# A two-block kernel on one core: expert fetches with a shorter lag, routing deferred, query columns in two parts

## The chip, the cores and the metric

The kernel runs on one core of one Trainium2 chip. The metric is the device time of one execution in microseconds (us). The engines are PE (matrix products), DVE (vector), ACT (scalar functions), POOL (which here mostly issues the indexed fetches) and SP (which issues the weight loads).

## The reference

Two transformer blocks over 256 tokens of 2048 channels, in float32. The change concerns the feed-forward part at the end of the first one, in which every token fetches 128 rows from each of two tables of 16384 rows:

```python
    q = (hf @ w_q).reshape(t, PEER_HEADS, 2, PEER_HALF).astype(jnp.float32)
...
    s1 = jnp.einsum('thd,nd->thn', q[:, :, 0], sk[0])
    s2 = jnp.einsum('thd,nd->thn', q[:, :, 1], sk[1])
    v1, i1 = lax.top_k(s1, PEER_TOPK)
    v2, i2 = lax.top_k(s2, PEER_TOPK)
    cand = (v1[..., :, None] + v2[..., None, :]).reshape(t, PEER_HEADS, PEER_TOPK * PEER_TOPK)
    cs, ci = lax.top_k(cand, PEER_TOPK)
    row = jnp.take_along_axis(i1, ci // PEER_TOPK, axis=-1)
    col = jnp.take_along_axis(i2, ci % PEER_TOPK, axis=-1)
    experts = row * PEER_NKEYS + col
    gates = jax.nn.softmax(cs, axis=-1)
...
        a = jax.nn.gelu(jnp.einsum('chkd,cd->chk', expert_u[ec], hc).astype(jnp.float32))
        w = (gc * a).astype(hc.dtype)
        return jnp.einsum('chk,chkd->cd', w, expert_v[ec])
```

Here `hf` is the normalized row (`h2` in the kernel), `w_q` is 2048 x 2048 (8 heads, two halves of 128 each), there are 128 keys to a half, PEER_TOPK is 16, and a row of `expert_u` or `expert_v` has 2048 floats. All of it is added to the residual, and the second block follows.

## The kernel before

Tokens stand on the 128 partitions, in two tiles t = 0 and 1. Every dense layer streams its weights in parts of 512 KB through four `raw` buffers (SP issues the loads in program order, `prep`, L106). ACT rounds a part to a high half (L109), DVE subtracts it to get the low half (L110), and PE makes each product of three of the faster float32r kind (L166 to L168): high x high, high x low, low x high. `h2` is kept in the same two halves, written by `split_evac` (L224 to L226). The four buffers that hold a split part are the `hl` buffers.

The first block ends with `w_out1`. Then comes `peer`: `w_qp` (the 2048 query columns) is a dense layer of 4 blocks of 512 columns, two heads to a block, 8 parts to a block. As a block ends, `ev_qp` evacuates it, transposes it (L216), multiplies it with the keys (L740) and gets 4 x 128 scores per token. For t = 0 the generator `route` follows at once, on DVE: top-16 of each 128 (L666 to L670), top-16 of the 256 sums, the row number in `ef` and, cast, in `eidx` (L717), the softmax, and a transposed copy of the row numbers in `eidv` (L680). For t = 1 the scores are kept in `gslot[:, 3]` and routed late. A generator that yields is resumed one part of the dense later (`tick`), so that DVE's rows of routing and of splitting alternate in its queue.

The fetches are indirect DMAs issued by POOL (L786), in the order of the list `seq`. A first-table fetch takes one row of `expert_u` for each of the 128 tokens of a tile (slot k of head and rank), 1 MiB; its use (`use_u`, L812) is a dot product with `hrow` on DVE, which frees the slot. When 32 are used, `weights` makes the coefficients. A second-table fetch brings, for four tokens, 32 rows each of `expert_v`; its use (`use_v`, L828) is four products on PE with 32 weight columns, whose strips of tokens accumulate over 128 fetches. `VLAG` is the number of first-table fetches that stand in `seq` before the first second-table fetch; from there the two kinds alternate.

A fetch needs a free slot and, for the first table, a routed head (`ready`). Slots before: `gslot` 0 to 2 and the tile `gbc` (the gain of `h2`, which `hrow` is made with at L659); after the dense the four `hl` buffers, and `gslot` 3 when the late scores are done. `hook` calls `step` (issue, use) before every second part of the dense. Every engine works off its queue in order; the order is fixed when the program is built.

Of the kernel before, what the change touches and what calls it, by code (L numbers as in the profile page):

```python
# [22 lines left out]
P = 128  # L23
T = 256
# [15 lines left out]
VLAG = 36  # L40


class Builder:
# [49 lines left out]
    def add_plan(self, w):  # L93
        nb, kc, _, kk, n = w.shape
        step = 2 if n <= 512 else 1
        for b in range(nb):
            for c in range(kc):
                for k0 in range(0, kk, step):
                    self.plan.append((w[b, c][:, k0:min(kk, k0 + step)], min(step, kk - k0), n))
# [134 lines left out]
    def row_to_lhs(self, row, HI, LO, kt, t, n=4, gain=None, scale=1.0):  # L234
        ps = self.transpose4(row, n)
        s = slice(t * P, (t + 1) * P)
        self.split_evac(ps, HI[:, kt:kt + n, s], LO[:, kt:kt + n, s],
                        None if gain is None else gain[:, kt:kt + n], scale)
# [73 lines left out]
    def build(self):  # L312
        nc, d = self.nc, self.d
        for w in ("w_ckvq", "w_kr", "w_ukv", "w_uq", "w_dqkv", "w_gate", "w_oa", "w_out1", "w_qp"):
# [5 lines left out]
            else:  # L320
                self.add_plan(d[w])
# [25 lines left out]
    def block1(self):  # L347
# [267 lines left out]
        h2h, h2l = self.pair("B", F32R, "h2")  # L615
        ss2 = cst.tile([P, 2, 4], F32, tag="ss2", name="ss2")

        def ev_out(b, t, ps):
# [5 lines left out]
            self.row_to_lhs(xres[:, t, sl], h2h, h2l, 4 * b, t, 4, G("g_norm2"))  # L624
# [3 lines left out]
        self.h2 = lambda k, t: (h2h[:, k, t * P:(t + 1) * P], h2l[:, k, t * P:(t + 1) * P])  # L628
        s2 = self.stat_sum(ss2, "r2")
# [4 lines left out]
    def peer(self):  # L634
# [6 lines left out]
        vmask = self.cload("vmask", [P, 8, 32], pool=pp)  # L641
# [33 lines left out]
        def spread(dst, src, b, copy):  # L675
            tp = self.tr()
            nc.tensor.transpose(tp[:, :P], src, self.ident)
            tv = tp[32 * b:32 * b + 32, :P].rearrange("p (i m) -> p m i", m=4)
            for m in range(4):
                copy(dst[32 * m:32 * m + 32], tv[:, m])  # L680

        def route(b, t, sc):
            sl = slice(32 * b, 32 * b + 32)
            V = rt(64, "rt_v").rearrange("p (h w s) -> p h w s", h=2, w=2)
            I = rt(64, "rt_i", U32).rearrange("p (h w s) -> p h w s", h=2, w=2)
            for j in range(4):
# [3 lines left out]
            tab = rt(64, "rt_tab").rearrange("p (h w s) -> p h w s", h=2, w=2)  # L690
            nc.vector.tensor_copy(tab, I)
            nc.vector.tensor_scalar(tab[:, :, 0], tab[:, :, 0], float(P), None, op0=ALU.mult)
            cand = self.at([P, 2, 16, 16])
            nc.vector.tensor_tensor(cand, V[:, :, 0].unsqueeze(3).to_broadcast([P, 2, 16, 16]),
                                    V[:, :, 1].unsqueeze(2).to_broadcast([P, 2, 16, 16]), op=ALU.add)
            cs = rt(32, "rt_cs")
            ci = rt(32, "rt_ci", U32)
            for i in range(2):
# [609 lines left out]
```

## Time and profile before

| | before |
|---|---|
| median of 3 runs | 2880.39 us (2880.06 to 2881.32) |
| the profiled execution | 2880.4 us, span 2878.6 us |
| PE, DVE, ACT, POOL busy, share of the span | 80%, 58%, 27%, 23% |
| mean granted clock of PE | 0.904 |
| moved by DMA | 820.24 MB, 285 GB/s mean |

Shares are means over the whole span, which holds stages of different limits: products from 0 to about 700 us and from 2062 us on, fetches in between. A row of the table by stretches gives the length, then the busy time and the number of instructions of PE, PE's weight loads, DVE, ACT and POOL, the granted clock (1.00 is 2.4 GHz), the share of the 16 DMA engines that is busy, and GB/s.

### The profile page before, as it was taken

What the parts mean: (1) busy time and instruction counts of PE and PEld (TensorE: products, weight loads), DVE (VectorE), ACT (ScalarE), POOL (GpSimd) and SP (SyncE); (2) the same over time, 40 slices, a digit from 0 to 9 for tenths busy, and PEclk for the clock granted to TensorE, in tenths of its full rate; (3) what the DMA queues carried; (4) which work ended last, traced back from release to release, by engine and by line L of the source; (5) the groups of instructions that cost most, each with busy time, mean ns of one, the idle gap of its engine ahead of it and who ended that gap; (6) DMA issues with size and microseconds to landing.
All of it is one profiled execution on the core that took longest, in us unless ns stands there. A gap on an engine that the chain in (4) does not pass through costs nothing.

```text
span 2878.6 us, 26351 instructions
## 1 busy us (share of the span) xinstructions
PE 2307.9 (80%) x9488; PEld 1445.4 (50%) x9488; DVE 1679.5 (58%) x2503; ACT 791.2 (27%) x1245; POOL 668.8 (23%) x570
## 2 busy tenths in 40 slices
PE   9999999999515565556666666657899999999999
PEld 7878788888401111111111111111388888888887
DVE  5665755657999644444445444441365566667754
ACT  6544544444200000000000000000244444447743
POOL 0000000000354554445445353534100000001000
PEclk9999999999857878887787878788999999999999
DMA  7545466555989999999999999999755555553355
GB/s 249 171 146 183 151 225 199 185 187 194 353 325 357 407 422 421 422 421 421 422 421 422 422 421 422 422 421 421 290 193 188 170 172 188 187 174 131 121 183 168
DMA packets 151955, 820.24 MB, mean 285 GB/s; under 512 B 17232, under 2 KB 17264, under 8 KB 85776
## 3 DMA queue, kind: packets, MB, share of 16 engines
q0 software_dynamic: 75360, 543.75, 46.1%
q1 hardware_dynamic: 76464, 274.81, 28.5%
q8 instruction: 74, 1.21, 0.2%
q14 instruction: 57, 0.47, 0.0%
HBM read 816.39 MB, written 2.10 MB: 284 GB/s over the span
## 4 chain that ended last, share of the span: by engine, by line
PE 50%; DMA 22%; issue 14%; DVE 7%; POOL 7%; ACT 0%; SPq 0%; POOLq 0%; DVEq 0%; ACTq 0%
PE acc L167 15%; PE acc L166 15%; PE acc L168 15%; DMA hg<-expert_v,eidv 8%; DMA gslot<-expert_v,eidv 7%; DMA hj<-expert_v,eidv 3%; POOL gslot L786 3%; POOL hg L786 3%; DVE hj L812 2%; DMA gslot<-expert_u,eidx 2%; PE tr L216 1%; PE acc L828 1%; POOL hj L786 1%; DVE hl L110 1%; PE sd L1146 1%
## 5 line engine op out<-in xcount | busy, mean ns | idle before, releaser
L110 DVE TENSOR_TENSOR hl<-raw,hl 128x1024 fp32r<-128x1024 f32 (+1 forms) x516 | 623.3, 1211 | 525.7 <-ACT hl L109 525.2
L109 ACT ACTIVATE hl<-raw 128x1024 fp32r<-128x1024 f32 (+1 forms) x516 | 540.9, 1049 | 765.9 <-PE acc L168 630.7
L166 PE MATMUL acc<-hl,h 128*128 128x512 f32 (+1 forms) x1472 | 580.8, 395 | 3.4 <-ACT hl L109 3.4
L167 PE MATMUL acc<-hl,h 128*128 128x512 f32 (+1 forms) x1472 | 574.4, 390 | 9.7 <-DVE hl L110 9.7
L168 PE MATMUL acc<-hl,h 128*128 128x512 f32 (+1 forms) x1472 | 573.7, 390 | 0.0
L828 PE MATMUL acc<-hg,lw 128*32 128x512 f32 x880 | 410.2, 811 | 199.5 <-DMA hg<-expert_v,eidv 195.7
L828 PE MATMUL acc<-gslot,lw 128*32 128x512 f32 x848 | 413.0, 806 | 176.2 <-DMA gslot<-expert_v,eidv 176.0
L812 DVE CUSTOM_DVE_ANT_0 hj<-gslot,hj 128x2048 f16<-128x2048 f32 x121 | 277.2, 2291 | 239.5 <-DMA gslot<-expert_u,eidx 239.2
L812 DVE CUSTOM_DVE_ANT_0 hj<-hg,hj 128x2048 f16<-128x2048 f32 x116 | 265.6, 2290 | 205.7 <-DMA hg<-expert_u,eidx 205.3
L167 PEld LDWEIGHTS acc<-hl,h 128*128 128x128 f32 x1472 | 277.1, 188 | 70.0 <-DVE hl L110 13.6
L166 PEld LDWEIGHTS acc<-hl,h 128*128 128x128 f32 x1472 | 276.8, 188 | 61.8 <-ACT hl L109 5.0
L168 PEld LDWEIGHTS acc<-hl,h 128*128 128x128 f32 x1472 | 276.7, 188 | 57.3 <-issue 1.3
L828 PEld LDWEIGHTS acc<-hg,lw 128*32 128x32 f32 x880 | 79.9, 139 | 442.5 <-DMA hg<-expert_v,eidv 273.2
L828 PEld LDWEIGHTS acc<-gslot,lw 128*32 128x32 f32 x848 | 80.3, 138 | 398.5 <-DMA gslot<-expert_v,eidv 251.4
L828 PE MATMUL acc<-hj,lw 128*32 128x512 f32 x320 | 208.1, 803 | 89.5 <-DMA hj<-expert_v,eidv 89.4
L799 ACT ACTIVATE dots<-dots 128x32 f32<-128x32 f32 x8 | 1.8, 229 | 985.7 <-DVE dots L812 985.7
L204 POOL TENSOR_TENSOR rs_y<-rs_v,mhalf 128x2 f32<-128x2 f32 (+2 forms) x25 | 30.3, 1213 | 809.8 <-DVE rs_v L203 809.2
L786 POOL DMA_INDIRECT hg<-expert_v,eidv x110 | 141.9, 1290 | 169.7 <-PE acc L828 126.2
L786 POOL DMA_INDIRECT gslot<-expert_v,eidv x106 | 129.5, 1222 | 205.1 <-PE acc L828 165.3
L786 POOL DMA_INDIRECT gslot<-expert_u,eidx x121 | 131.3, 1085 | 184.6 <-issue 71.9
L786 POOL DMA_INDIRECT hg<-expert_u,eidx x116 | 138.8, 1196 | 128.6 <-DMA hg<-expert_v,eidv 29.1
L828 PEld LDWEIGHTS acc<-hj,lw 128*32 128x32 f32 x320 | 39.7, 139 | 194.1 <-DMA hj<-expert_v,eidv 118.9
(304 smaller groups left out, 2377.1 us busy)
## 6 DMA issues: line engine op xcount, KB each, us to landing
raw<-ev_in SPq DMA_DIRECT2D x128, 512.0 KB, 4.5
raw<-od_in SPq DMA_DIRECT2D x72, 512.0 KB, 3.8
raw<-w_gate SPq DMA_DIRECT2D x64, 512.0 KB, 4.3
raw<-w_dqkv SPq DMA_DIRECT2D x48, 512.0 KB, 3.5
raw<-w_out SPq DMA_DIRECT2D x32, 512.0 KB, 3.8
raw<-w_qp SPq DMA_DIRECT2D x32, 512.0 KB, 5.0
raw<-ev_out SPq DMA_DIRECT2D x32, 512.0 KB, 4.3
raw<-od_out SPq DMA_DIRECT2D x32, 512.0 KB, 4.5
```

Source lines behind the costliest of these rows:

```text
L109: nc.scalar.activation(hi, raw, AF.Copy)
L110: nc.vector.tensor_tensor(lo, raw, hi.bitcast(F32), op=ALU.subtract)
L166: nc.tensor.matmul(o, xh, wh, start=start, stop=False)
L167: nc.tensor.matmul(o, xh, wl, start=False, stop=False)
L168: nc.tensor.matmul(o, xl, wh, start=False, stop=stop)
L204: nc.gpsimd.tensor_tensor(y, v, self.mhalf[:, :n], op=ALU.pow)
L216: self.nc.tensor.transpose(ps[:, j * P:(j + 1) * P], row[:, j * P:(j + 1) * P], self.ident)
L786: nc.gpsimd.indirect_dma_start(out=g[0], out_offset=None, in_=d[table], in_offset=bass.IndirectOffsetOnAxis(ap=ix, axis=0))
L799: nc.scalar.activation(dots[:, t, sl], dots[:, t, sl], AF.Gelu_apprx_tanh)
L812: nc.vector.tensor_tensor_reduce(junk, g[0], hrow[:, t], 1.0, 0.0, op0=ALU.mult, op1=ALU.add, accum_out=dots[:, t, k:k + 1])
L828: nc.tensor.matmul(st["acc"][n][32 * q:32 * q + 32], lws[t, b][:, q, i], g[0][:, n * 512:(n + 1) * 512], start=(x % P < 4), stop=(x % P >= ...
L1146: nc.tensor.matmul(o, pT[:, i * (t + 1) + k], vo[:, k, g * 64:(g + 1) * 64], start=(k == 0), stop=(k == t))
```

## The change

The second table's fetches follow the first's after 20 instead of 36, and the coefficients are made for 16 fetches at a time. The query columns are split. The first 512, now `w_qa`, are a dense layer of two blocks of 256 columns (one head each), still in three split products, in 8 parts. The other 1536, `w_qp`, are three blocks in 24 parts that are not split: one plain float32 product straight from the `raw` buffer, with an unsplit copy of `h2` that lies in `gslot` 0 and 1. `route` handles one or two heads; head 0 of t = 0 is routed as soon as its scores stand, without a pause, and its 16 columns are `ready` at once. All other scores are kept, and their routes run one at a time, started between uses. The transposed copies are made with a masked multiplication (L702) and one product with a constant (L708) instead of a transpose and four copies. `hrow` is made inside the dense of `w_qa` (`rows`). Slots: `gslot` 2 and `gbc` first, the four `hl` buffers after `w_qa`, `gslot` 0 and 1 after `w_qp`, `gslot` 3 later.

```diff
-VLAG = 36
+VLAG = 20
...
         while self.nprep < min(upto, self.limit, len(self.plan)):
-            src, ks, n = self.plan[self.nprep]
+            src, ks, n, whole = self.plan[self.nprep]
             raw = self.rawp.tile([P, ks, n], F32, tag="raw", name="raw")
             nc.sync.dma_start(raw, src)
+            if whole:
+                self.ready[self.nprep] = [(raw[:, k], None) for k in range(ks)]
+                self.nprep += 1
+                continue
...
     def products(self, o, xh, xl, wh, wl, start, stop):
         nc = self.nc
+        if wl is None:
+            nc.tensor.matmul(o, xh, wh, start=start, stop=stop)
+            return
...
+        h2w = self.gslot[:, 0:2].rearrange("p a (k t) -> p (a k) t", t=T)
...
-        for t in range(2):
-            nc.vector.scalar_tensor_tensor(hrow[:, t], xres[:, t], r2[:, t:t + 1], gbc, op0=ALU.mult, op1=ALU.mult)
-        gslot = self.slot("G", [P, 4, D], name="gslot")
-        sc1 = gslot[:, 3].rearrange("p (b c) -> p b c", b=4)
-        free = deque([(gslot[:, i], False) for i in range(3)] + [(gbc, False)])
+        def rows():
+            for t in range(2):
+                nc.vector.scalar_tensor_tensor(hrow[:, t], xres[:, t], r2[:, t:t + 1], gbc, op0=ALU.mult, op1=ALU.mult)
+            free.append((gbc, False))
...
+        order = [(h, n, t) for t in range(2) for h, n in ((0, 1), (1, 1), (2, 2), (4, 2), (6, 2))][1:]
...
+        free = deque([(gslot[:, i], False) for i in range(2, 3)])
...
+        def spread(L):
+            ps = self.tr()[:, :16]
+            nc.tensor.matmul(ps, L.rearrange("p m s -> p (m s)"), tdiv, start=True, stop=True)
+            return ps
...
+            if first:
+                todo = route(h0, nh, t, ps, True)
+                while ready[t] == 0:
+                    next(todo)
+                yield 1
+                yield from todo
+            else:
+                nc.scalar.activation(score[h0, t], ps, AF.Copy)
+                have.add((h0, t))
...
+        def route_next(use):
+            if late and st["use"] >= use and late[0][::2] in have and not any(x[3] == "late" for x in self.tasks):
+                h, nh, t = late.popleft()
+                self.spawn(route(h, nh, t, score[h, t]), "late")
...
         def hook():
             n[0] += 1
-            if n[0] % 2 == 0:
+            if n[0] == 3:
+                rows()
+            if n[0] > 8 or n[0] % 2 == 0:
                 step()
+            if len(late) == len(order):
+                route_next(4)
 
         self.hook = hook
-        self.dense(d["w_qp"], self.h2, ev_qp, rate=0.0)
-        self.hook = None
+        self.dense(d["w_qa"], self.h2, ev_qa, rate=0.0)
         for _ in range(4):
             free.append((self.hlp.tile([P, D], F32, tag="hl", name="hg"), True))
-        late = [0, 1, 2, 3]
+        self.dense(d["w_qp"], self.h2w, ev_qp, rate=0.0)
+        self.hook = None
+        for i in range(2):
+            free.append((gslot[:, i], False))
```

The order shows three places. The first is DVE at the end of the first route, up to the cast of the row numbers (`eidx`) for which POOL's first fetch waits. Before:

```order
544 L669 MAX rt_cs<-at 128x8 [waits DVE_49]
545 L110 TENSOR_TENSOR hl<-raw,hl 128x1024 [waits DMAHW4_49,Activation_49]
546 L670 MAX_INDEX rt_ci<-rt_cs,at 128x8 [waits DVE_49]
...
552 L709 TENSOR_TENSOR hj<-rt_f,io 128x1024 [waits DVE_49]
553 L110 TENSOR_TENSOR hl<-raw,hl 128x1024 [waits DMAHW5_49,Activation_49]
554 L714 TENSOR_TENSOR hj<-hj,rt_tab 128x1024 [waits DVE_49]
555 L726 RECIPROCAL s_5583<-s_5583 128x2
556 L716 TENSOR_REDUCE ef<-hj 128x32 [waits DVE_49]
557 L110 TENSOR_TENSOR hl<-raw,hl 128x1024 [waits DMAHW6_49,PE_49,Activation_49]
558 L717 CAST eidx<-ef 128x32 [waits DVE_49]
```

Of the change, the same place (L739 is L709 of before, L747 is L717, L865 is the dot product L812):

```order
525 L739 TENSOR_TENSOR hj<-rt_f,io 128x512 [waits DVE_49]
526 L762 RECIPROCAL s_5396<-s_5396 128x1 [waits DVE_49]
527 L744 TENSOR_TENSOR hj<-hj,rt_tab 128x512 [waits DVE_49]
528 L763 TENSOR_TENSOR gate<-gate,s_5396 128x16 [waits DVE_49]
529 L746 TENSOR_REDUCE ef<-hj 128x16 [waits DVE_49]
530 L747 CAST eidx<-ef 128x16 [waits DVE_49]
531 L702 SCALAR_TENSOR_TENSOR at<-ef,tmod 128x128 [waits DMASW7_49]
532 L759 CAST eidv<-tr 128x16 [waits PE_49]
533 L865 ISA hj,dots<-gslot,hj 128x2048 [waits DMASW1_49]
```

The splits of weight parts (L110) between the rows of the route are gone, and the tiles are half as wide. The second place is POOL's queue at the first fetches. Before:

```order
32 L786 DMA gslot<-expert_u,eidx 128x2048 [waits DMASW7_49,DVE_49,PE_49]
33 L786 DMA gslot<-expert_u,eidx 128x2048 x2
34 L786 DMA hj<-expert_u,eidx 128x2048 [waits DMAHW1_49,PE_49]
35 L786 DMA gslot<-expert_u,eidx 128x2048 [waits DMASW7_49,DVE_49]
36 L786 DMA gslot<-expert_u,eidx 128x2048 [waits DMASW0_49,DVE_49]
```

Four slots (`gslot` 0 to 2, and `gbc`, which the order calls `hj`) are filled before the first is used again. The same place in the change, where `hg` is an `hl` buffer:

```order
34 L838 DMA gslot<-expert_u,eidx 128x2048 [waits DVE_49,PE_49]
35 L838 DMA hj<-expert_u,eidx 128x2048 [waits DMAHW1_49,PE_49,Activation_49]
36 L838 DMA hg<-expert_u,eidx 128x2048 [waits PE_49,Activation_49]
37 L838 DMA gslot<-expert_u,eidx 128x2048 [waits DMASW1_49,DVE_49]
38 L838 DMA hj<-expert_u,eidx 128x2048 [waits DMASW5_49,DMASW2_49,DVE_49]
39 L838 DMA hg<-expert_u,eidx 128x2048 [waits DMASW6_49,PE_49,Activation_49]
```

Now three are filled, the fourth fetch waits for the first use, and the other `hl` buffers come behind it in the queue. The third place is PE in the dense of `w_qp`. Before, at the end of it:

```order
3112 L166 MATMUL acc<-hl,h_4464 128x512 [waits Activation_49]
3113 L167 MATMUL acc<-hl,h_4464 128x512 [waits DVE_49]
3114 L168 MATMUL acc<-hl,h_4464 128x512
3115 L166 MATMUL acc<-hl,h_4464 128x512
3116 L167 MATMUL acc<-hl,h_4464 128x512
```

Each part begins with waits for ACT and for DVE, and has 12 such products. Of the change, in the second block, around the spreading of head 0's coefficients (L708):

```order
3080 L171 MATMUL acc<-raw,gslot 128x512 [waits DMAHW2_49]
3081 L171 MATMUL acc<-raw,gslot 128x512
3082 L708 MATMUL tr<-tdiv,at 128x16 [waits DVE_49,PE_49]
3083 L171 MATMUL acc<-raw,gslot 128x512 x2
3084 L171 MATMUL acc<-raw,gslot 128x512 [waits DMAHW3_49]
3085 L171 MATMUL acc<-raw,gslot 128x512 x3
```

A part now waits for its load alone and has 4 products, and in part 16 of 24 stands a product that waits for DVE's 16th use. The first products of the second table follow after part 20; before, they stand behind the whole dense.

## Rows read from the trace of the kernel before

**Rows 1.** Table by stretches of the stage of the fetches.
```profile
692.00:714.00 22.00, 22.00 (x108) 18.43 (x108) 21.50 (x67) 10.50 (x14) 0.00 (x0) 1.00 0.53 177
714.00:720.00 6.00, 6.00 (x35) 5.13 (x33) 4.25 (x14) 2.05 (x3) 3.89 (x4) 1.00 0.65 194
720.00:740.00 20.00, 18.32 (x87) 14.89 (x86) 15.49 (x38) 7.65 (x9) 4.83 (x4) 1.00 0.98 389
740.00:760.00 20.00, 14.78 (x74) 11.54 (x73) 19.86 (x52) 6.43 (x9) 4.44 (x4) 1.00 0.72 252
760.00:800.00 40.00, 8.41 (x37) 6.16 (x35) 38.12 (x76) 2.20 (x4) 22.44 (x15) 0.65 1.00 395
800.00:860.00 60.00, 7.92 (x25) 4.96 (x25) 59.83 (x134) 4.96 (x10) 29.19 (x18) 0.50 0.86 320
860.00:960.00 100.00, 56.62 (x142) 11.40 (x143) 96.32 (x272) 2.20 (x5) 53.66 (x37) 0.78 0.92 358
960.00:1960.00 1000.00, 606.82 (x1632) 128.63 (x1628) 479.25 (x436) 11.15 (x42) 472.76 (x402) 0.80 1.01 422
...
2040.00:2062.00 22.00, 15.51 (x61) 3.84 (x62) 2.66 (x4) 1.04 (x3) 3.58 (x4) 0.92 0.75 289
...
2062.00:2878.60 816.60, 809.16 (x3866) 667.45 (x3864) 509.01 (x845) 399.21 (x633) 28.93 (x27) 1.00 0.51 170
```

**Rows 2.** Timeline of POOL: start, length, instruction, [idle before <-releaser].
```profile
715.20 1.31 POOL L786 DMA_INDIRECT gslot<-expert_u,eidx  x1 [50.28 <-issue]
...
787.60 3.00 POOL L786 DMA_INDIRECT hj<-expert_u,eidx  x1 [1.77 <-DVE s L725]
...
847.65 2.17 POOL L786 DMA_INDIRECT hg<-expert_v,eidv  x1 [0.31 <-issue]
...
2053.38 0.94 POOL L786 DMA_INDIRECT hj<-expert_v,eidv  x1 [5.64 <-PE acc L828]
```

**Rows 3.** Timeline of DVE from the row multiplication to the first index cast.
```profile
670.26 4.62 DVE L659 SCALAR_TENSOR_TENSOR hj<-xres,r,hj 128x2048 f32<-128x2048 f32 x2 [2.31 <-DMA hj<-g_norm]
...
677.13 0.68 DVE L226 TENSOR_TENSOR h<-at,h 128x512 fp32r<-128x512 f32 x1
...
692.36 0.30 DVE L666 MAX8 rt_v<-sd 128x8 f32<-128x128 f32 x1 [1.78 <-PE sd L740]
...
714.16 0.17 DVE L717 CAST eidx<-ef 128x32 uint32<-128x32 f32 x1
```

**Rows 4.** Timeline of PE: split products of 320 and 512 columns, second-table products.
```profile
58.61 0.30 PE L166 MATMUL acc<-hl,h 128*128 128x320 f32 x1
58.76 0.31 PE L167 MATMUL acc<-hl,h 128*128 128x320 f32 x1
...
685.33 0.39 PE L166 MATMUL acc<-hl,h 128*128 128x512 f32 x1
685.56 0.39 PE L167 MATMUL acc<-hl,h 128*128 128x512 f32 x1
...
1999.49 0.59 PE L828 MATMUL acc<-hj,lw 128*32 128x512 f32 x1
...
1999.92 0.59 PE L828 MATMUL acc<-hj,lw 128*32 128x512 f32 x1
...
2059.01 0.62 PE L828 MATMUL acc<-hj,lw 128*32 128x512 f32 x1 [1.35 <-DMA hj<-expert_v,eidv]
```

**Rows 5.** Groups of DVE's instructions from 715 to 960 us: busy us, mean ns.
```profile
L812 DVE CUSTOM_DVE_ANT_0 hj<-gslot,hj 128x2048 f16<-128x2048 f32 x27 | 61.7, 2283 | 8.9 <-DMA gslot<-expert_u,eidx 8.8
...
L110 DVE TENSOR_TENSOR hl<-raw,hl 128x1024 fp32r<-128x1024 f32 x12 | 14.5, 1212 | 0.0
...
L812 DVE DVE_READ_ACCUMULATOR2_ANT dots<- 128x1 f32 x54 | 4.6, 86 | 0.0
```

**Rows 6.** DMA issues from 715 to 2062 us: count, KB each, median us to landing.
```profile
raw<-w_qp SPq DMA_DIRECT2D x8, 512.0 KB, 7.6
raw<-ev_in SPq DMA_DIRECT2D x8, 512.0 KB, 8.2
```

More of the change, by code (lines that the diff above doesn't have):

```diff
@@ L320, in build @@
             else:
-                self.add_plan(d[w])
+                self.add_plan(d[w], whole=w == "w_qp")
         self.limit = len(self.plan)
@@ L673, in rt, with masked, route @@
             return pp.tile([P, n], dt, tag=tag, name=tag, bufs=2)
[L675 to L686, printed above, removed]
+        def masked(src, bias):
+            L = self.at([P, 8, 16])
+            nc.vector.scalar_tensor_tensor(L, src.unsqueeze(1).to_broadcast([P, 8, 16]), bias,
+                                           tmod.unsqueeze(2).to_broadcast([P, 8, 16]), op0=ALU.add, op1=ALU.mult)
+            return L
+        def spread(L):
+            ps = self.tr()[:, :16]
+            nc.tensor.matmul(ps, L.rearrange("p m s -> p (m s)"), tdiv, start=True, stop=True)
+            return ps
+        def route(h0, nh, t, sc, hurry=False):
+            n = 16 * nh
+            sl = slice(16 * h0, 16 * h0 + n)
+            V = rt(64, "rt_v")[:, :2 * n].rearrange("p (h w s) -> p h w s", h=nh, w=2)
+            I = rt(64, "rt_i", U32)[:, :2 * n].rearrange("p (h w s) -> p h w s", h=nh, w=2)
+            for j in range(2 * nh):
                 tmp = self.at([P, P])
@@ L720, in route @@
             c = cs.rearrange("p (h s) -> p h s", s=16)
-            nc.vector.tensor_tensor(gv, c, c[:, :, 0:1].to_broadcast([P, 2, 16]), op=ALU.subtract)
+            nc.vector.tensor_tensor(gv, c, c[:, :, 0:1].to_broadcast([P, nh, 16]), op=ALU.subtract)
             nc.scalar.activation(gate[:, t, sl], gate[:, t, sl], AF.Exp)
-            spread(eidv[:, t, sl], ef[:, t], b, nc.vector.tensor_copy)
-            s2 = self.small(2, "s2")
+            halves = [slice(16 * (h0 + h), 16 * (h0 + h) + 16) for h in range(nh)]
@@ L725, in route @@
+            Ls = [masked(ef[:, t, sh], 0.25) for sh in halves]
+            yield 1
+            for sh, L in zip(halves, Ls):
+                nc.vector.tensor_copy(eidv[:, t, sh], spread(L))
+            s2 = self.small(2, "s2")[:, :nh]
             nc.vector.tensor_reduce(s2, gv, axis=AX.X, op=ALU.add)
             nc.vector.reciprocal(s2, s2)
-            nc.vector.tensor_tensor(gv, gv, s2.unsqueeze(2).to_broadcast([P, 2, 16]), op=ALU.mult)
-            ready[t] = 32 * b + 32
-        def ev_qp(b, t, ps):
-            row = self.ev()
-            nc.scalar.activation(row, ps, AF.Copy, scale=r2[:, t:t + 1])
-            yield 1 + t
-            tp = self.transpose4(row)
-            qT = self.at([P, 4, P])
-            nc.scalar.activation(qT, tp, AF.Copy)
-            yield 1
-            ps = self.sd()
-            for j in range(4):
-                nc.tensor.matmul(ps[:, j * P:(j + 1) * P], qT[:, j], sk[:, j % 2], start=True, stop=True)
-            if t == 0:
-                yield from route(b, t, ps)
-            else:
-                nc.scalar.activation(sc1[:, b], ps, AF.Copy)
+            nc.vector.tensor_tensor(gv, gv, s2.unsqueeze(2).to_broadcast([P, nh, 16]), op=ALU.mult)
@@ new lines, in route, with ev_q @@
+            ready[t] = 16 * h0 + n
+        def ev_q(h0, nh, t, ps):
+            first = h0 + t == 0
+            row = self.ev()[:, :256 * nh]
+            nc.scalar.activation(row, ps, AF.Copy, scale=r2[:, t:t + 1])
+            if not first:
+                yield 1 + t
+            tp = self.transpose4(row, 2 * nh)
+            qT = self.at([P, 4, P])[:, :2 * nh]
+            nc.scalar.activation(qT, tp, AF.Copy)
+            if not first:
+                yield 1
+            ps = self.sd()[:, :256 * nh]
+            for j in range(2 * nh):
+                nc.tensor.matmul(ps[:, j * P:(j + 1) * P], qT[:, j], sk[:, j % 2], start=True, stop=True)
+            if first:
+                todo = route(h0, nh, t, ps, True)
+                while ready[t] == 0:
+                    next(todo)
+                yield 1
+                yield from todo
+            else:
+                nc.scalar.activation(score[h0, t], ps, AF.Copy)
+                have.add((h0, t))
@@ L1237, in consts @@
     out["kdec"] = np.ascontiguousarray((np.exp(lg[None, :] * (127.0 - i[:, None])) / 16.0).astype(f))
-    vm = np.zeros((4, 32, 8, 32), f)
-    for m in range(4):
-        for i_ in range(8):
-            vm[m, :, i_, 4 * i_ + m] = 1.0
-    out["vmask"] = vm.reshape(P, 8, 32)
+    vm = np.zeros((8, 16, 4, 32), f)
+    for m in range(8):
+        for i_ in range(4):
+            vm[m, :, i_, 8 * i_ + m] = 1.0
+    out["vmask"] = vm.reshape(P, 4, 32)
+    out["tmod"] = np.ascontiguousarray((i[:, None] % 8 == np.arange(8)[None, :]).astype(f))
+    out["tdiv"] = np.ascontiguousarray((i[:, None] // 8 == np.arange(16)[None, :]).astype(f))
     return out
```

107 lines of the change are left out of this document (63 added, 44 removed).

## The prediction

> **What bounds the kernel now.** I read first the table by stretches [rows 1]. From 960 to 1960 us the DMA engines are full (share 1.01, 422 GB/s) while DVE works 479 us of 1000 and PE 607: a stretch set by transfers. It belongs to the 512 fetches of expert rows, 256 from each table, each 128 x 2048 floats, 1.049 MB. At 422 GB/s one takes 2.486 us, all of them 1272.8. Next I looked for the ends of this stream in POOL's timeline [rows 2]: the first fetch goes out at 715.20, the last at 2053.38, and PE starts on the last one's data at 2059.01 [rows 4]. What follows (2062 to 2878.6, DMA at 170 GB/s) is untouched by the change. So the kernel's time is 2880.4 (span 2878.6) as long as the stream ends at 2059; whatever moves that moves the total one to one.
>
> The end is a sum: start + fetches + weights that travel inside the stream + idle DMA time. Eight parts of w_qp and eight of ev_in are issued between the first fetch and the end [rows 6]; one is 0.524 MB, 1.24 us, together 19.8. The idle time is worked out per stretch as length x (1 - GB/s / 422) [rows 1]: 3.2 (714 to 720), 1.6, 8.1, 2.6, 14.5, 15.2 (860 to 960), together 45; and 7 at the end (2040 to 2062). 715.2 + 1272.8 + 19.8 + 45 + 7 = 2059.8, against 2059.0 read. The sum holds to 1 us, and I use it for the change.
>
> Why is DMA idle from 714 to 960? DVE is busy 19.86 of 20, 38.12 of 40, 59.83 of 60 and 96.32 of 100 us there [rows 1]. One dot product of a fetched row (L812) costs it 2.283 + 0.086 us [rows 5], against 2.486 for the fetch: with first-table fetches alone DVE is 95% taken before it routes anything. Routing and the splits of the weights (L110, 12 x 1.212 = 14.5 us) [rows 5] come on top, slots come free late, and POOL has nothing to issue into. The first second-table fetch, which costs DVE nothing, leaves only at 847.65 [rows 2].
>
> **The change, part by part.**
>
> *The start.* Before, the first top-16 runs at 692.36 and the index cast ends it at 714.16 + 0.17; POOL fetches at 715.20 [rows 2, 3]. Three things shorten this. (a) The first block is 256 columns wide. A split product of 512 columns starts every 0.227 us, one of 320 every 0.147 [rows 4]; that extrapolates to 0.12 for 256. Its 96 products take 11.5 us where 512 columns took 21.8. But the last quarter of K needs the last part of h2. Before, both row multiplications (L659, 4.62 us from 670.26, when their DMA has landed) stand ahead of it, and it is done at 677.8 [rows 3]. Now one of them, 2.31 us, stays ahead, so I put it at 676, the block's end at 678 (685.6 before, [rows 4]), and with the same chain of evacuation, transposes and key products, which also loses its pauses (7 us before, I take 5), the first top-16 at 683. (b) One head is routed, not two: the 21.9 us contain 8 splits of 1.21, so two heads cost some 12 and one about 8, since short dependent operations do not halve. (c) No split stands between its rows, as the DVE order shows. Cast at 691, first fetch at **692** (bounds 688, if h2 holds nothing up, and 700, if one head costs what two did and 4 us more are lost). Gain 23.2 us.
>
> *The weights.* w_qp no longer all travels ahead of the stream. Of its 24 parts four fit into the raw buffers before 692; the other 20, not 8, lie inside the stream: 12 x 1.24 = **+14.9 us**. Between 18 and 22 parts this is 12.4 to 17.4.
>
> *Plain products.* The unsplit product of 512 columns appears before as L828 with 32 weight columns: two records each, 0.43 apart, so 0.86 us [rows 4], against 3 x 0.227 = 0.68. For 96 products that is 83 us, from about 691 to 774 or later; DVE loses 24 splits (29 us), ACT 24 copies. PE is not on the path so long as the scores of heads 2 and 3 come in time. DVE asks for them after 11 uses, about 692 + 9 (landing) + 11 x 3.6 = 741 (a fetch and its share of weights together take 3.6). PE has them after 10 parts, 691 + 34 + 5 = 730. That is 11 us of slack. PE then meets the spreading product of head 0 in the middle of part 16, at about 744, and must wait there for the 16th use, near 757. This delays the later parts by some 13 us; heads 4 and 5 are wanted after 26 uses, near 790, and come near 772. Both covers hold on these numbers; if they go, DVE waits in order with uses behind it, POOL with full slots behind that.
>
> *Idle time.* What made 45 us of it is removed in two ways. From u20 on every other fetch is free for DVE, so a pair costs it 2.37 of 4.97 us; and the splits are gone. Routing stays (some 12 us per two heads), and is spread by the order over the later uses. From 692 to 790 I count about 24 uses (57 us) and 29 us of routing, masks and weights: 86 of 98, below full, where before it was full. I keep 4 us for the start (only three slots are issued before the fourth fetch waits for the first use, as the POOL order shows), 8 for two queues running together (389 instead of 422 GB/s from 720 to 740 [rows 1], over some 95 us), 8 for waits in order: **20 in place of 45**. The bounds are 8 (start and a little mixing) and 45 (all as before). I take the value nearer the lower, since after 960, with both kinds of fetch and 8 or 9 slots, there is none [rows 1]. The tail's 7 stay.
>
> *POOL's issues.* The same 512. One takes 0.94 us, but 3.00 where a dot product runs beside it [rows 2]; over the full stretch 402 take 472.76, 1.18 each [rows 1]. By the long row alone an issue would cost more than the 2.486 of its transfer; by the mean it costs nothing, and I take the mean, since that stretch has as many uses per us as the new one will. The Trainium skill, "SBUF — State Buffer", section "SBUF: two separate sides", says that a DVE operation with two SBUF inputs, or in a two-port mode, and a GpSimd operation exclude each other for the whole instruction, so that descriptors wait; the 3.00 agrees with it, the mean of 1.18 shows that it is rarely met, and by that rule taken fully the sum would be the last rival's below.
>
> **Sum.** 692 + 1272.8 + 28 x 1.24 + 20 + 7 = 2026.5, against 2059.8: -23.2 + 14.9 - 25 = -33.3. 2880.4 - 33.3 = **2847 us** (the profiled 2880.4 equals the median, 2880.39). Likeliest's own range 2834 to 2859.
>
> **Rivals.**
> 1. *DVE stays the bound.* If the route of one head after the other fills DVE as before and idle stays at 45, the end is at 2051.5 and the time 2872. For: DVE at 88% by my count, in order. Against: 29 us less splitting. Everything between, 2859 to 2872, belongs here.
> 2. *The start does not move* (the block waits for h2, the chain for its pauses). With the first fetch at 715, only 8 parts of w_qp are left inside: -25 us alone, 2855; with half the relief 2868.
> 3. *Slower: PE at the low clock.* PE waits for head 0's dots near 744. When PE had little to do (8.41 of 40 us from 760 to 800) the granted clock was 0.65, then 0.50, that is 1.2 GHz [rows 1]. Were the whole plain dense to run so, a part would take 6.9 us: heads 2 and 3 at 765 instead of 741, the first second-table use (after part 20) near 829, and POOL, whose slots hold five second-table fetches by then, stands still some 48 us in all. Idle 20 + 48 = 68 gives 2895. It decides from 53 us of idle on (45 - 14.9 + 23.2 = 53.3 for no change). Against: at 692 to 714 PE is busy 22.00 of 22 at clock 1.00, and the new dense is as full until 744.
> 4. *Issue locked out.* If each issue until routing is done cost 3.0 + 0.3 instead of 2.486, the first 80 or so would lose 0.8 each, 64 us, less the idle counted already: 2880 to 2891. Against: the mean of 1.18.
>
> **Chances.** Forecast 0.58; rival 1 0.25; rival 2 0.06; rival 3 0.08; rival 4 0.03. The measurement of this kernel tells about 0.2% (5.8 us) from no change, so faster is below 2874.6: the first three, 0.88 with a small loss to the edge, 0.87. Within 0.2%: edges of rivals 1 and 4, 0.05. Slower 0.08. The range reaches down to 2832 (idle 8 and start 690) and up to 2870, into rival 1; it leaves out some 2 in 10.
>
> **What would show it.** First fetch issued at 692; the first top-16 at 683 with no split before the cast. In 700 to 960 GB/s near 400 and DVE under 95% in 700 to 790, some 70% after. Plain products 0.86 apart at clock 1.00 until 744, then a wait for DVE of some 13 us. First second-table fetch near 756 (847.65 before). Stream ends near 2026, and what lies behind it is still 816.6 us long. I am wrong if DVE is full again up to 900, if PE's clock falls to 0.5 during the dense, or if DVE waits for scores with fetched rows behind it.

## The result and the profile after

The changed kernel takes 2844.53 us (median of 4 runs, 2842.43 to 2847.86) against 2880.22 (4 runs); the ratio is 0.9877, 95% interval 0.986 to 0.9894. The profiled execution is its slowest, 2847.86 us with a span of 2846.1, 32.5 less than the one of before. The forecast was 2847, range 2832 to 2870.

The stretches first, to be held against [rows 1] (length, busy and instructions of PE, weight loads, DVE, ACT, POOL, then clock, DMA share, GB/s):

```profile
700.00:720.00 20.00, 15.32 (x40) 6.81 (x38) 19.10 (x47) 0.60 (x2) 6.93 (x8) 0.98 1.01 414
720.00:740.00 20.00, 20.00 (x59) 10.41 (x60) 15.80 (x29) 3.17 (x6) 14.69 (x7) 0.85 1.01 418
740.00:760.00 20.00, 18.64 (x46) 8.14 (x45) 14.32 (x16) 3.37 (x5) 5.07 (x6) 1.00 1.02 417
760.00:780.00 20.00, 16.94 (x60) 8.31 (x59) 12.24 (x26) 2.29 (x4) 4.68 (x5) 1.00 1.01 416
780.00:800.00 20.00, 20.00 (x50) 6.84 (x49) 5.88 (x11) 1.37 (x2) 1.87 (x2) 1.00 0.90 371
800.00:830.00 30.00, 17.52 (x72) 5.68 (x70) 23.23 (x61) 5.08 (x7) 16.61 (x15) 0.83 0.93 361
...
860.00:900.00 40.00, 23.81 (x62) 5.31 (x64) 35.61 (x92) 1.74 (x3) 18.62 (x16) 0.79 0.94 373
900.00:960.00 60.00, 34.48 (x96) 7.42 (x94) 41.52 (x103) 1.72 (x3) 30.93 (x23) 0.84 0.99 398
960.00:1960.00 1000.00, 614.52 (x1656) 133.61 (x1652) 527.41 (x647) 15.18 (x33) 481.53 (x402) 0.79 1.01 420
...
2028.00:2846.00 818.00, 810.04 (x3870) 667.53 (x3866) 509.53 (x846) 399.74 (x635) 28.91 (x27) 1.00 0.51 170
```

From 700 to 780 us the DMA engines are full (414 to 418 GB/s, 252 to 395 in the like stretches of before), and DVE has time to spare from 720 on. Most of the idle time that is left, 14.7 of 26.5 us, lies between 780 and 960. Behind the stream nothing changed.

The start in DVE's timeline (compare [rows 3]):

```profile
670.08 2.35 DVE L674 SCALAR_TENSOR_TENSOR hj<-xres,r,hj 128x2048 f32<-128x2048 f32 x1 [0.93 <-DMA hj<-g_norm]
...
680.76 0.29 DVE L691 MAX8 rt_v<-sd 128x8 f32<-128x128 f32 x1
...
689.02 0.18 DVE L747 CAST eidx<-ef 128x16 uint32<-128x16 f32 x1
...
804.49 0.09 DVE L693 MATCH_VALUE_LOAD at<-rt_v,gslot 128x8 f32 x1 [12.70 <-PE sd L779]
```

The first top-16 runs at 680.76 instead of 692.36 and the cast comes 8.3 us later instead of 21.8. The last row is a wait that the prediction did not have; more of it below. DVE's load, which the prediction counted as 86 of the 98 us from 692 to 790:

```profile
692.00:790.00 98.00, 88.89 (x248) 41.02 (x246) 67.95 (x119) 10.46 (x19) 34.61 (x28) 0.97 1.01 411
```

The ends of the stream in POOL's timeline (compare [rows 2]):

```profile
690.08 1.07 POOL L838 DMA_INDIRECT gslot<-expert_u,eidx  x1 [22.86 <-PE tr L708]
...
752.62 0.94 POOL L838 DMA_INDIRECT hj<-expert_v,eidv  x1 [2.82 <-DVE dots L865]
...
2018.47 0.94 POOL L838 DMA_INDIRECT hj<-expert_v,eidv  x1 [3.57 <-PE acc L881]
```

And PE's timeline, the plain dense, its two waits for DVE, and the last fetch (compare [rows 4]):

```profile
701.33 13.90 PE L171 MATMUL acc<-raw,gslot 128*128 128x512 f32 x32
719.91 0.61 PE L708 MATMUL tr<-tdiv,at 128*128 128x16 f32 x2 [4.68 <-DVE at L702]
720.36 9.98 PE L171 MATMUL acc<-raw,gslot 128*128 128x512 f32 x16
...
756.68 0.37 PE L708 MATMUL tr<-tdiv,at 128*128 128x16 f32 x2 [1.36 <-DVE at L702]
...
2025.88 0.62 PE L881 MATMUL acc<-hj,lw 128*32 128x512 f32 x1 [1.38 <-DMA hj<-expert_v,eidv]
```

32 records are 16 products; in 13.90 us that is 0.87 each. The 8 products from 720.36 on take 9.98 us, 3 more than at that rate. The last fetch is used at 2025.88, 33.1 earlier than before.

### The profile page after: what moved, and what is told of

It reads as the page before. It is cut to its first block, busy times and chain, and to the rows that moved or that the text cites. A ratio compares the mean times of both kernels' runs of the same rounds, so it can differ in the third digit from the quotient of the medians.

```text
span 2846.1 us, 26398 instructions
## 1 busy us (share of the span) xinstructions
PE 2352.4 (83%) x9536; PEld 1442.6 (51%) x9536; DVE 1666.1 (59%) x2539; ACT 775.2 (27%) x1216; POOL 659.0 (23%) x572
## 4 chain that ended last, share of the span: by engine, by line
PE 51%; DMA 25%; issue 12%; POOL 7%; DVE 4%; ACT 0%; SPq 0%; POOLq 0%; DVEq 0%; ACTq 0%
PE acc L174 15%; PE acc L173 15%; PE acc L175 15%; DMA hg<-expert_v,eidv 11%; DMA gslot<-expert_v,eidv 8%; POOL hg L838 3%; POOL gslot L838 2%; PE acc L881 2%; DMA gslot<-expert_u,eidx 2%; DMA hj<-expert_u,eidx 2%; DVE hj L865 1%; PE tr L223 1%; POOL hj L838 1%; PE sd L1209 1%; DMA hg<-expert_u,eidx 1%
## 5 line engine op out<-in xcount | busy, mean ns | idle before, releaser
L114 DVE TENSOR_TENSOR hl<-raw,hl 128x1024 fp32r<-128x1024 f32 (+1 forms) x492 | 593.6, 1210 | 480.1 <-ACT hl L113 479.6
L881 PE MATMUL acc<-hg,lw 128*32 128x512 f32 x1080 | 500.9, 830 | 268.4 <-DMA hg<-expert_v,eidv 266.9
L173 PE MATMUL acc<-hl,h 128*128 128x512 f32 (+2 forms) x1408 | 548.3, 390 | 3.3 <-ACT hl L113 3.0
L174 PE MATMUL acc<-hl,h 128*128 128x512 f32 (+2 forms) x1408 | 542.8, 386 | 4.1 <-DVE hl L114 4.1
L175 PE MATMUL acc<-hl,h 128*128 128x512 f32 (+2 forms) x1408 | 542.0, 385 | 0.0
L865 DVE CUSTOM_DVE_ANT_0 hj<-gslot,hj 128x2048 f16<-128x2048 f32 x105 | 240.5, 2290 | 187.4 <-DMA gslot<-expert_u,eidx 186.8
L174 PEld LDWEIGHTS acc<-hl,h 128*128 128x128 f32 x1408 | 265.7, 189 | 57.7 <-DVE hl L114 6.3
L173 PEld LDWEIGHTS acc<-hl,h 128*128 128x128 f32 x1408 | 265.1, 188 | 57.3 <-ACT hl L113 4.3
L175 PEld LDWEIGHTS acc<-hl,h 128*128 128x128 f32 x1408 | 265.5, 189 | 52.8 <-issue 1.3
L865 DVE CUSTOM_DVE_ANT_0 hj<-hg,hj 128x2048 f16<-128x2048 f32 x92 | 210.6, 2289 | 134.4 <-DMA hg<-expert_u,eidx 134.2
L838 POOL DMA_INDIRECT hg<-expert_v,eidv x135 | 171.1, 1267 | 222.7 <-PE acc L881 162.5
L865 DVE CUSTOM_DVE_ANT_0 hj<-hj 128x2048 f16<-128x2048 f32 x59 | 135.1, 2291 | 127.1 <-DMA hj<-expert_u,eidx 127.0
L838 POOL DMA_INDIRECT hg<-expert_u,eidx x92 | 106.6, 1158 | 71.8 <-DVE dots L865 26.6
L171 PE MATMUL acc<-raw,gslot 128*128 128x512 f32 x192 | 88.5, 611 | 0.0
```

Of the source, the lines that this page charges most:

```text
L114: nc.vector.tensor_tensor(lo, raw, hi.bitcast(F32), op=ALU.subtract)
L171: nc.tensor.matmul(o, xh, wh, start=start, stop=stop)
L174: nc.tensor.matmul(o, xh, wl, start=False, stop=False)
L175: nc.tensor.matmul(o, xl, wh, start=False, stop=stop)
L838: nc.gpsimd.indirect_dma_start(out=g[0], out_offset=None, in_=d[table], in_offset=bass.IndirectOffsetOnAxis(ap=ix, axis=0))
L865: nc.vector.tensor_tensor_reduce(junk, g[0], hrow[:, t], 1.0, 0.0, op0=ALU.mult, op1=ALU.add, accum_out=dots[:, t, k:k + 1])
```

## The experiments

All are built from the changed kernel. For each I took the sum that the prediction uses: first fetch + 1272.8 + 1.24 per weight part issued inside the stream + idle time, length x (1 - GB/s / 422) over 13 or so stretches between the first fetch and the last use. (With these finer edges the kernel before has 50.0 us of idle time, not 52.) The table holds one profiled execution of each; the medians are of 4 to 5 runs.

| kernel | first fetch | parts | idle | sum | last fetch used | median us | ratio to before |
|---|---|---|---|---|---|---|---|
| before | 715.2 | 16 | 50.0 | 2057.8 | 2059.0 | 2880.22 | 1 |
| changed | 690.1 | 28 | 26.5 | 2024.1 | 2025.9 | 2844.53 | 0.9877 (0.986 to 0.9894) |
| lag 36 | 687.8 | 28 | 31.4 | 2026.7 | 2027.6 | 2849.38 | 0.989 (0.9874 to 0.9907) |
| w_qp split | 692.4 | 23 | 29.6 | 2023.4 | 2026.4 | 2851.7 | 0.9897 (0.9881 to 0.9914) |
| one block | 704.0 | 24 | 23.0 | 2029.5 | 2033.8 | 2853.95 | 0.9902 (0.9886 to 0.9919) |
| queries elsewhere | 686.6 | 28 | 27.1 | 2021.2 | 2020.9 | 2843.3 | 0.9867 (0.985 to 0.9883) |
| lag 36 and split | 693.0 | 23 | 38.7 | 2033.0 | 2036.4 | 2858.31 | 0.9923 (0.9906 to 0.9939) |
| spaced routes | 687.4 | 28 | 28.7 | 2023.6 | 2024.6 | 2845.22 | 0.988 (0.986 to 0.99) |
| 20 parts not loaded | 686.3 | 8 | 43.3 | 2012.3 | 2013.2 | 2834.35 | 0.9833 (0.9816 to 0.9849) |
| routed at once | 687.0 | 28 | 28.4 | 2022.9 | 2025.1 | 2849.63 | 0.9894 (0.9878 to 0.9911) |
| half the products | 688.9 | 28 | 29.9 | 2026.3 | 2027.9 | 2848.95 | 0.9883 (0.9867 to 0.9898) |
| half, not loaded | 688.0 | 8 | 31.5 | 2002.2 | 2002.1 | 2819.39 | 0.9779 (0.9764 to 0.9795) |
| DVE in program order | 688.2 | 28 | 22.9 | 2018.6 | 2018.6 | 2839.97 | 0.9852 (0.9838 to 0.9866) |
| changed, again | 686.9 | 28 | 22.7 | 2017.1 | 2018.3 | 2843.19 | 0.9869 (0.9853 to 0.9884) |

The sum meets the end within 4.3 us in all fourteen, within 2 in ten. It nearly has to: the idle time is what the moved bytes leave of the time, so the sum tests only that nothing but the fetches and the counted parts was moved. That the stream sets the kernel's time is seen behind it: from the use of the last fetch to the end of the span it is 818.8 to 820.3 us in all fourteen profiles.

The table also shows the scatter. The changed kernel's two profiles differ by 3.2 us at the start, 3.8 in idle time and 7.6 at the end, so that less than some 8 us between two single profiles is not resolved. The medians are steadier: the changed kernel's two differ by 1.3, and the kernel before, run beside each group, gave 2880.22 to 2882.12. Only "lag 36 and split" and the two runs without loads have intervals clear of both of the changed kernel's; "one block" is clear of one of them. Where only medians differ, by 5 to 7 us, the difference is likely, not shown.

**The lag back at 36.**

```diff
-VLAG = 20
+VLAG = 36
...
-                route_next(VLAG - 2)
+                route_next(18)
```

> The changed kernel with the lag back at 36 and nothing else undone (late routes still start after 18 uses). Theory A (the end of the fetches is start + fetches + weights + idle DMA time; idle went because DVE is relieved both by the missing splits and by the earlier second-table fetches): start unchanged at 690, DVE full again between about 770 and 840, some 10 us of idle time back, 2855 (2850 to 2860). Rival B (the shorter lag alone took the idle away): all 23 us back, 2867. Rival C (only the missing splits count): 2845, as changed.

+4.9 us by the medians, just below A's range and above C, with an interval that overlaps the changed kernel's. The table by stretches shows one hole, and POOL's timeline what it is:

```profile
800.00:830.00 30.00, 1.59 (x6) 1.43 (x6) 29.36 (x90) 1.73 (x3) 11.98 (x8) 0.50 0.47 182
```

```profile
786.16 0.94 POOL L838 DMA_INDIRECT hg<-expert_u,eidx  x1 [2.84 <-DVE dots L865]
815.88 0.94 POOL L838 DMA_INDIRECT gslot<-expert_u,eidx  x1 [28.79 <-DVE s L762]
```

The 33rd first-table fetch needs the index cast of heads 2 and 3, which DVE, busy 29.36 of 30 us, reaches at 814.95:

```profile
814.95 0.16 DVE L747 CAST eidx<-ef 128x32 uint32<-128x32 f32 x1
```

So the shorter lag works less by making DVE cheaper per fetch than by time: the second-table fetches keep DMA busy while the next heads are routed. Of the 31.4 us of idle time 17.1 lie in this one hole; the same stretch lost 4.3 us in the changed kernel.

**w_qp split again.**

```diff
-                self.add_plan(d[w], whole=w == "w_qp")
+                self.add_plan(d[w], whole=False)
...
-        free = deque([(gslot[:, i], False) for i in range(2, 3)])
+        free = deque([(gslot[:, i], False) for i in range(3)])
...
-        for _ in range(4):
-            free.append((self.hlp.tile([P, D], F32, tag="hl", name="hg"), True))
-        self.dense(d["w_qp"], self.h2w, ev_qp, rate=0.0)
+        self.dense(d["w_qp"], self.h2, ev_qp, rate=0.0)
         self.hook = None
-        for i in range(2):
-            free.append((gslot[:, i], False))
+        for _ in range(4):
+            free.append((self.hlp.tile([P, D], F32, tag="hl", name="hg"), True))
```

> The changed kernel with w_qp split again into high and low halves, three fast products each (the 24 splits back on ACT and DVE); the slots follow from it: three of gslot and the gain's tile from the start, the four split buffers only after the dense. Theory A: DVE gets 24 x 1.21 = 29 us more between 690 and 760 and has only 4 slots there, so 10 to 20 us of idle time come back and the first cast is a few us later: 2860 (2853 to 2868). Rival B (the lag alone): 2846. Rival C (the splits alone): 2868 or more.

+7.2 us by the medians, again less than A had. The first fetch is 2 to 5 us later, 3 us of idle time come back, and five parts of weights fewer lie inside the stream. In the sum these cancel, and the 7.2 us do not show: the profiled execution, 2847.02, is the fastest of its four, that of the changed kernel the slowest of its own. What the profile does show is the route: five splits stand between its first top-16 (677.75) and the cast (691.40), 13.7 us instead of 8.3.

**Both.** The two edits together.

> Both undone: lag 36 and w_qp split again (with the slots that go with it). Each alone cost 5 to 7 us. Theory A2 (DVE's two reliefs cover for each other: with either, DVE keeps up; with neither, it is full as before the change): the idle time returns to some 45 us, 2866 (2860 to 2872). Rival D (the two add up, and what took the idle away is the deferred routing, one route at a time): 2856 (2853 to 2859).

+13.8 us, nearer to the sum of the two (12.0) than to the return of all idle time: A2 fell. The hole of lag 36 is there again (18.7 us from 800 to 830), and 38.7 of the 50.0 us of before. Some 11 us of the relief are therefore in neither of the two edits. The uses show where to look: DVE starts the 16th dot product 81.5 us after the first fetch before the change, and 60.5 after it here, although the lag, the splits and the slots are those of before.

```profile
796.68 2.29 DVE L812 CUSTOM_DVE_ANT_0 hj<-hg,hj 128x2048 f16<-128x2048 f32 x1
```

```profile
753.49 2.28 DVE L865 CUSTOM_DVE_ANT_0 hj<-hj 128x2048 f16<-128x2048 f32 x1
```

The first row is of the kernel before, the second of this run. Left in it, besides the single first head that the run with one block undoes, are the deferred routes, the coefficients for 16 fetches, the masked multiplication, and `step` before every part after the eighth, where the kernel before has it before every second part. Only the deferral was undone, next, and alone; which of them it is stays open.

**Routed at once.** The list of late routes holds the second tile's only, and none is started inside the dense.

```diff
-            if first:
+            if t == 0 and not first:
+                yield from route(h0, nh, t, ps)
+            elif first:
                 todo = route(h0, nh, t, ps, True)
...
-                route_next(VLAG - 2)
+                if ready[0] == P:
+                    route_next(VLAG + 4)
```

> The changed kernel with the routes of all heads of the first tile run at once as their scores come, up to two at a time, as before the change; only the second tile's are deferred. Theory A2: DVE's load is the same, only bunched earlier, where it has 10 to 15% to spare: 2848 (2844 to 2853). Rival D (the deferral is what took the idle time away): 2862 or more.

+5.1 us by the medians, with idle time as in the changed kernel (28.4 against 26.5) in a profile whose own time was the lowest of its runs, 2845.76. D fell; how much the deferral is worth beyond the scatter, or with the other two edits undone as well, stays open.

**One block of two heads.**

```diff
-        order = [(h, n, t) for t in range(2) for h, n in ((0, 1), (1, 1), (2, 2), (4, 2), (6, 2))][1:]
+        order = [(h, n, t) for t in range(2) for h, n in ((0, 2), (2, 2), (4, 2), (6, 2))][1:]
...
-            return ev_q(b, 1, t, ps)
+            return ev_q(0, 2, t, ps)
...
-    o["w_qa"] = pack(a["w_q_peer"][0][:, :512], n=256)
+    o["w_qa"] = pack(a["w_q_peer"][0][:, :512])
```

> The changed kernel with the first 512 query columns as one block of two heads, routed together at once, without pauses. Theory A: the block ends some 8 us later and two heads take about 12 instead of 8 us to route, so the first fetch goes out at 702 to 704 instead of 690; three parts of weights fewer lie behind it (-4), one route fewer stands among the uses: 2853 (2849 to 2857). Rival (the start does not matter, since DVE has to catch up anyway): 2845.

2853.95, as A had it, +9.4. DVE's and POOL's timelines of this run:

```profile
688.73 0.30 DVE L691 MAX8 rt_v<-sd 128x8 f32<-128x128 f32 x1 [9.50 <-PE sd L779]
...
702.92 0.18 DVE L747 CAST eidx<-ef 128x32 uint32<-128x32 f32 x1
```

```profile
703.97 1.07 POOL L838 DMA_INDIRECT gslot<-expert_u,eidx  x1 [37.49 <-DVE eidv L759]
```

Of the later start the block's width makes 8.0 us (688.73 against 680.76, give or take the 3 us of scatter at the start), the second head in the route 5.9 (14.2 us to the cast against 8.3). A later start, in part paid by four parts fewer in the stream, moves the end.

**20 parts not loaded.** After the fourth part of `w_qp` the buffers are used again as they are.

```diff
+            if whole and len(self.kept) == 4:
+                raw = self.kept[self.nprep % 4]
+                self.ready[self.nprep] = [(raw[:, k], None) for k in range(ks)]
+                self.nprep += 1
+                continue
```

> The changed kernel with only the first 4 of the 24 parts of w_qp loaded; the other 20 products use these four again, so the queries of heads 2 to 7 are not the reference's, and rows fetched for them are others, as many. Theory A (weights inside the stream cost their transfer time, since DMA is the bound): -20 x 1.24 = -24.8 us, less some 5 for DVE, which then has to keep up with faster first fetches: 2822 (2819 to 2830). Rival (the weights travel in time that is idle anyway, DVE bounds the first 100 us): 2842 or more.

-10.2 instead of -24.8 less 5. The weights do cost time, but not all that their bytes would give back. POOL's timeline has the rest:

```profile
770.02 0.94 POOL L845 DMA_INDIRECT gslot<-expert_v,eidv  x1 [0.30 <-DVE rt_i L702]
789.02 0.94 POOL L845 DMA_INDIRECT hj<-expert_u,eidx  x1 [18.05 <-PE acc L888]
```

Slots full of second-table rows wait for PE, whose products for them stand among the plain products of the dense. That was a guess, and the next two runs tested it.

**Half the products, with and without the loads.**

```diff
                     for t in range(2):
+                        if wl is None and k % 2:
+                            continue
```

> The changed kernel with every second product of w_qp left out (the queries of heads 2 to 7 sum only half of the channels, so other rows are fetched for them, as many); all 24 parts are still loaded. The dense takes PE 41 instead of 83 us. Theory A (the plain products lie off the path, as the prediction had it): 2844 (2842 to 2847). Theory P (PE's dense is late for the last scores and for the first second-table products, which is the wait of 12.70 us at 804): the idle time between 780 and 830, 6.7 us, goes: 2838 (2835 to 2841).

> The run without 20 of the weight parts, and with every second product of w_qp left out as well. Theory P (without the loads the fetches run ahead of PE's dense, and the 15 us of idle time between 740 and 800 come from that): idle falls from 43 to 28, 2820 (2816 to 2825). Rival (DVE is the bound of that stretch without the loads): 2832.

With the loads, halving PE's work gains nothing: 2848.95 against 2843.19 for the changed kernel beside it, longer than either theory had it. That does not show that PE's dense is off the path, since another wait came in its place. ACT's and DVE's timelines of this run:

```profile
771.26 0.69 ACT L771 ACTIVATE ev<-acc,r 128x512 f32<-128x512 f32 x1 [29.36 <-PE acc L171]
...
774.97 0.22 ACT L853 ACTIVATE dots<-dots 128x16 f32<-128x16 f32 x1
```

```profile
775.22 0.17 DVE L854 TENSOR_TENSOR dots<-dots,gate 128x16 f32<-128x16 f32 x1 [15.99 <-ACT dots L853]
```

ACT's function of head 0's dots (L853) stands here behind the evacuation of the last query block (L771), which waits for PE and its loads; in the changed kernel it ran at 752.38, before the evacuation of the second block. DVE waited 15.99 us with fetched rows behind it (its next four dot products wait for nothing), and from 780 to 800 the DMA engines moved 244 GB/s (371 in the changed kernel). What the dense costs beside the loads stays open.

Without the loads halving the products gains 15.0 (2834.35 to 2819.39), as theory P had it, and idle time falls from 43.3 to 31.5. Against the changed kernel that is 23.8 us for 20 parts, whose bytes are 24.8. By these two runs the dense is the next limit, some 10 us behind the loads: in the changed kernel DMA carries weights and fetches at 414 to 418 GB/s until 780, and PE's plain products end near 799.

**The waits that are left.** The 12.70 us at 804 are a scratch buffer that the key product of the last heads still reads. First the transposed queries were moved out of the scratch pool:

```diff
-            qT = self.at([P, 4, P])[:, :2 * nh]
+            qT = self.ev().rearrange("p (k t) -> p k t", t=P)[:, :2 * nh]
```

> The changed kernel with the transposed queries in a buffer of the evacuation pool (6) instead of the scratch pool (3). In the changed kernel DVE waits 12.70 us at 804 for a scratch buffer that a key product on PE still reads, which stands behind second-table products. Theory A: that wait goes, 5 to 7 us of idle time between 780 and 830 with it: 2839 (2837 to 2842). Rival (the time is made up later, since slots were full anyway, or another wait takes its place): 2844.

The rival was right. The wait is gone, and DVE's next row in line waits longer, for the scores themselves:

```profile
800.70 0.49 DVE L691 MAX8 rt_v<-gslot 128x8 f32<-128x128 f32 x2 [13.67 <-ACT gslot L787]
```

Then the routes were spaced:

```diff
-                route_next(VLAG - 2)
+                if late:
+                    u = 128 * late[0][2] + 16 * late[0][0] - 28
+                    route_next(max(VLAG - 2, 2 * u - VLAG))
```

> The version with the transposed queries in the evacuation pool, and in addition each late route is started only when the first-table uses are within 28 of its first row, instead of one right after the other. There DVE waited 13.67 us at 787 for the scores of heads 6 and 7, which nobody needs until the 96th use. Theory A: that wait and the bunched routes up to 1100 go, 6 to 9 us of idle time with them: 2836 (2833 to 2839). Rival (the ninth slot, which holds scores and comes free later this way, costs as much as the waits): 2843.

No gain, and a wait of 16.44 us for a score at 804: the scheduler, which is free to order DVE, had put the first top-16 of the later heads ahead of uses, whatever the program's order. With DVE's order fixed as well, and the route of heads 2 and 3 started inside the dense:

```diff
-        with self.tc.manual_schedule(engines={mybir.EngineType.PE, mybir.EngineType.Pool}):
+        with self.tc.manual_schedule(engines={mybir.EngineType.PE, mybir.EngineType.Pool, mybir.EngineType.DVE}):
...
-            if len(late) == len(order):
+            if len(late) >= len(order) - 1:
                 route_next(4)
```

> The spaced version, with DVE's instructions too kept in the order in which the program issues them while the fetches run (in the spaced run the scheduler had moved the first top-16 of later heads ahead, and DVE waited 16.44 us at 804 for their scores); the route of heads 2 and 3 starts inside the dense. Theory A: no wait for a score before it is needed, idle 7 to 9 us less: 2837 (2833 to 2840). Rival (dependent steps of a route, now without other work between them, and PE's order cost as much): 2845.

2839.97, five runs from 2837.87 to 2841.32, against 2843.19 (2838.95 to 2847.6) for the changed kernel beside it. The long waits for scores and scratch buffers are gone, DVE's longest is now for a fetched row, and the medians go the expected way, but half as far, and the intervals of the ratios overlap: a gain of 3 us is likely, not shown.

```profile
805.68 2.29 DVE L865 CUSTOM_DVE_ANT_0 hj<-hj 128x2048 f16<-128x2048 f32 x1 [17.00 <-DMA hj<-expert_u,eidx]
```

> The changed kernel itself once more, beside the others on the same chip, as the base for differences of a few us: 2844.5 (2842 to 2848).

The repeat gave 2843.19, ratio 0.9869 (0.9853 to 0.9884).

## Why the prediction was right, step by step

**The frame held.** Whatever moved the last use of a fetch moved the kernel's end with it, 818.8 to 820.3 us behind it in all fourteen profiles. That the sums meet the end is no proof of more, as said above: they divide the time into terms, and what moves a term must come from the runs. The 7 us of the tail hold 3 in which the stream was over (2059 to 2062); up to the last use it is 4.2 before and after, so the difference does not suffer. The chances of the forecast and of rivals 1 and 2 add up to 0.89, not 0.88.

**The start**: forecast 692, gain 23.2; measured 690.08, gain 25.1, with the top-16 at 680.76 (683 forecast) and the route at 8.3 us (8 forecast). The narrow block (8.0 us) and the single head (5.9) are seen in the run with one block, the missing splits in the run with w_qp split (13.7 us of route instead of 8.3).

**The weights**: 20 parts inside the stream, as forecast. By their bytes the 12 added ones are +14.9 us; no run took away these 12 alone. Sparing all 20 gave back 10.2 of 24.8 us, since PE follows, and 23.8 with PE's products halved as well.

**The idle time**: 20 forecast before the tail, 22.3 measured (26.5 with the 4.2 after 1960). The total is right, its parts are not. For two queues together I had 8 us; from 700 to 780 it cost 1.1. For waits in order I had 8; from 780 to 960 they cost 14.7, and another 3.4 come after 960, where I had none. Two mis-sized terms cancelled, which was luck. The 389 GB/s of [rows 1], which I read as two queues disturbing each other, was not the price of two queues, since the same two moved 418 here.

**The mechanism behind it** was half right. I expected the shorter lag and the missing splits to account for the relief; undone together they bring back 12 of the 23.5 us. The lag's share comes from routing in time, not from DVE's load per fetch. The other 11 have no cause that a run shows. DVE's count was off too: of the 98 us from 692 to 790 it was busy 67.95, not 86. The uses were the 24 that I counted; most of the routing came later: from 860 to 900 DVE was busy 35.61 of 40 us, with 4.6 of the idle time there.

**PE's waits**: I forecast 13 us at 744 for head 0's dots. They came at 756.68 and lasted 1.36, because PE had already lost 4.68 us to head 1's spreading product, which I had not priced, and ran at a granted clock of 0.85 from 720 to 740, which made 8 products 3 us longer; most of the rest are transposes and key products between the parts. The slack of 11 us for the scores of heads 2 and 3 was used up: DVE was there at 733.60 instead of 741 and waited 2.16 for them. The wait of 12.70 us for a buffer behind the last scores I had overlooked: I counted when scores are asked for, not which buffers their operands hold. A row whose fetch was issued at 785.71 had landed at 795.78, in the middle of that wait, and was used only after it; POOL waited 9.69 us for PE to free a slot:

```profile
801.29 0.94 POOL L838 DMA_INDIRECT hj<-expert_u,eidx  x1 [9.69 <-PE acc L881]
```

So the sign by which I said that I would be wrong, DVE waiting for scores with fetched rows behind it, did come, with a score product in the way, and PE was on the path there. The 6.7 us of idle time from 780 to 830 were small enough to stay within the 20.

**The rivals.** Rival 3 (low clock) did not come: 0.85 is the lowest of the 20 us stretches of the dense. Rival 4 (issues locked out): from 720 to 740 an issue took 14.69 / 7 = 2.1 us, more than twice the short one, with 418 GB/s moved all the same, so the long issues hide behind transfers in flight. What makes them long is in the trace:

```profile
719.77 2.29 DVE L865 CUSTOM_DVE_ANT_0 hj<-hg,hj 128x2048 f16<-128x2048 f32 x1
719.85 3.02 POOL L838 DMA_INDIRECT hg<-expert_u,eidx  x1 [1.87 <-DVE eidx L747]
```

The issue ends at 722.87, 0.81 us after the dot product (722.06). From 960 to 1960 us the same holds for all 109 issues, of 402, that start while a dot product runs: they end 0.81 to 0.89 us after it. The 258 that start while DVE does nothing take 0.94. So about one issue in four meets such a wait, which I took for rare from the mean of 1.18; these 109 average 1.89 us, and the mean over all 402 is still 1.20. The Trainium skill, "SBUF — State Buffer", section "SBUF: two separate sides", describes such an exclusion, for a DVE operation with two SBUF inputs only against a GpSimd operation that reads SBUF. The trace agrees: the dot product has two inputs (`hg`, `hj`), and the issue reads its row numbers from `eidx`. From 720 to 740 it cost no time.

## What to carry to other kernels

Where one resource is full for most of a stage, write the stage's end as a sum (start, bytes that must pass, bytes that travel along, idle time) and make it meet the profile before using it (which proves the count of the bytes, not the cause); a change is then read term by term, and bytes moved into the stage count against an earlier start. Look for the resource next in line before counting on a saved term: the weights' 25 us gave back 10 until PE's share was cut as well. And see to what each full slot or scratch buffer waits for in every queue: taking away one wait for the last scores only showed the next one.

## What was not expected of the hardware

Two DMA queues at once, weight loads and indexed fetches, moved 414 to 418 GB/s over 80 us, 98 to 99% of the 422 of the fetches alone. An indirect DMA issued while a dot product ran on DVE was finished 0.81 to 0.89 us after that product, 109 times out of 109. The granted clock of PE fell to 0.85 in a stretch in which PE was busy 20.00 of 20 us, after a wait of 4.68 (0.50 from 719.9 to 726, 1.00 from there to 740); in the run with lag 36 it fell to 0.50, the lower level of 1.2 GHz, in a stretch in which PE was busy 1.59 of 30.
